# Three forms of an MLP's first product, and hidden layers cut in four pieces at twelve places, in a two-block transformer kernel

## The chip, the cores and the metric

The program runs on one core of one Trainium2 chip. The metric is the device time of one execution in microseconds (us); lower is better. The times below are of whole executions; the profile is of one more execution, whose instructions were recorded.

## The reference

Two transformer blocks in a row, on 256 tokens of width 1024, all in float32: the first with sparse attention, a linear recurrence and a short convolution, then the second with two layers, each an attention mixer and an MLP. So the program has three MLPs, and the change is in them and in where their operands lie. Cut to what matters:

```python
D_MODEL, SEQ, D_FF = 1024, 256, 4096

def first_block(x, ...):
    ...                                   # mixers, then x = x + mixed @ w_out
    h = _rmsnorm(x, ln_mlp_g)
    return x + jnp.square(jax.nn.relu(h @ w_mlp_up)) @ w_mlp_down

def second_block(x, ...):
    for layer in range(2):
        h = rmsnorm(x, norm_mix[layer])
        x = x + (even_mixer, odd_mixer)[layer](h, ...)
        h = rmsnorm(x, norm_mlp[layer])
        x = x + jnp.square(jax.nn.relu(h @ w_up[layer])) @ w_down[layer]
    return rmsnorm(x, norm_final)
```

## The kernel before

**Arithmetic.** Every large product is done in three parts: weights W and activations a are each split into a rounded high part (float32r) and the rest, and W·a is taken as h·ah + h·al + l·ah (h, l the parts of the weights, ah, al those of the activations). Activations lie transposed: 128 partitions by k (8 blocks of 128 for the width 1024, 32 for 4096) by 256 tokens. One matrix multiplication (matmul) takes a 128x128 block of weights as its stationary side and 256 or 512 columns of activations as its moving side.

**Weights.** They come from memory as one stream `w` in chunks of 16 blocks. `take` (L183) splits a unit of 8 blocks: ScalarE (ACT) writes `whi` (L193), VectorE (DVE) writes `wlo` in two halves (L195). Each of `whi` and `wlo` has five buffers of one unit, at fixed addresses.

**Forms of a product.** `gemm` (L246) makes one output tile of 128x256 with three matmuls for each k: L250 (h·ah), L253 (h·al), L254 (l·ah). `gemm2` makes two such tiles in one buffer `pg` of PSUM; there are four `pg`. `gemm_wide` (L257) has two matmuls for each k: L262 takes al behind ah as 512 columns in one matmul, L263 adds l·ah on 256 columns. The two halves of its result are then added: ACT copies one out (L412), DVE adds (L413).

**An MLP** (`mlp`, L379). First product: 32 output tiles, in 16 pairs by `gemm2` from `xo` (`xh`, `xl`), 8 k each; each pair goes through L395 (relu, ACT), L396 (square to the high part of `hid`, ACT), L397 and L398 (DVE: the low part of `hid`). Second product: 8 output tiles of 32 k from `hid`, seven by `gemm_wide`, the last by `gemm`. So each product has 256 steps of one k for one output tile. Before the first product `variance` (L380) sums squares into the one buffer `po` by matmuls (L347, L348), and DVE reads it (L382, L383). The three MLPs are called with `gain_next` = "norm_mix0" (the first block's), "norm_mix1" and `None`: here the first, second and third MLP.

**Places.** `xo` and `hid` are one tile each, with 128 elements more than they need (`ROOM`), and what is written into them starts some elements behind the tile's beginning: `PLACES` gives that for `xo` in each stage, `HIDDEN` for `hid` in each MLP. The tiles' own addresses do not change, so these numbers set how far the moving columns lie from the weights' buffers. In the stages named: "block1" is the first block's mixer, "ln_mlp_g" the first MLP's first product, "norm_mix0" the mixer behind it, "norm_mlp0" the second MLP, "norm_mix1" the last mixer, "norm_mlp1" the third MLP.

**Order.** Each engine works through its own queue in order. A scheduler that simulates the engines sets that order when the program is built.

Of the kernel before, what the change touches and what calls it, by code (L numbers as in the profile page):

```python
# [10 lines left out]
FP32 = mybir.dt.float32  # L11
FP32R = mybir.dt.float32r
# [3 lines left out]
ALU = mybir.AluOpType  # L16
# [27 lines left out]
ROOM = 128  # L44
PLACES = {"block1": 32, "ln_mlp_g": 64, "norm_mix0": 24, "norm_mlp0": 96, "norm_mix1": 20, "norm_mlp1": 0}
HIDDEN = {"norm_mix0": 16, "norm_mix1": 48, None: 8}
MIXED = 16
# [35 lines left out]
def kernel(  # L83
# [42 lines left out]
    def place(stage):  # L126

        nonlocal xh, xl
        at = PLACES[stage]
        xh, xl = placed(xo, KD, at), placed(xo, KD, at + KD * T)  # L130

# [110 lines left out]
    def drain():  # L242
        while due or chains:
            slot()

    def gemm(ps, ks, ah, al, prev=None):  # L246

        for k in ks:
            h, l = block()
            m0 = nc.tensor.matmul(out=ps, lhsT=h, rhs=ah[:, k], start=(k == ks[0]), stop=False)  # L250
            if k == ks[0]:
                after(m0, prev)
            nc.tensor.matmul(out=ps, lhsT=h, rhs=al[:, k], start=False, stop=False)  # L253
            m1 = nc.tensor.matmul(out=ps, lhsT=l, rhs=ah[:, k], start=False, stop=(k == ks[-1]))  # L254
        return m1

    def gemm_wide(kt, a):  # L257

        ps = pg_p.tile([128, 2, T], FP32, name="pg")
        for k in range(kt):  # L260
            h, l = block()
            nc.tensor.matmul(out=ps, lhsT=h, rhs=a[:, k], start=(k == 0), stop=False)  # L262
            nc.tensor.matmul(out=ps[:, 1], lhsT=l, rhs=a[:, k, 0], start=False, stop=(k == kt - 1))  # L263
        slot(kt / KD)
        return ps
# [100 lines left out]
    def residual(ah, al, groups, gain):  # L366


        for ks in groups[:-1]:
            for j in range(KD):  # L370
                nc.vector.tensor_tensor(out=x[:, j], in0=gemm1(ks, ah, al, RC), in1=x[:, j], op=ALU.add)
        drain()
        place(gain)
        for j in range(KD):
            nc.vector.tensor_tensor(out=x[:, j], in0=gemm1(groups[-1], ah, al), in1=x[:, j], op=ALU.add)
            operand(j, gain)
            squares(j)

    def mlp(gain_next):  # L379
        def variance():  # L380
# [5 lines left out]
        with ExitStack() as st:  # L386
            hp = pool("hid", stack=st)
            mp = pool("mlpt", 2, stack=st)
            hid = hp.tile([128, FF // 128 * 2 * T + ROOM], FP32R, name="hid")
            hid = placed(hid, FF // 128 * 2, HIDDEN[gain_next]).rearrange("p (k i) t -> p k i t", i=2)  # L390
            for j in range(0, FF // 128, 2):
                ps = gemm2(KD, xh, xl)
                r = mp.tile([128, 2, T], FP32, name="r")
                s = mp.tile([128, 2, T], FP32, name="s")
                nc.scalar.activation(out=r, in_=ps, func=AF.Relu)  # L395
                nc.scalar.activation(out=hid[:, j:j + 2, 0], in_=r, func=AF.Square)  # L396
                nc.vector.scalar_tensor_tensor(out=s, in0=ps, scalar=0.0, in1=r, op0=ALU.max, op1=ALU.mult)  # L397
                nc.vector.tensor_tensor(out=hid[:, j:j + 2, 1], in0=s, in1=hid[:, j:j + 2, 0], op=ALU.subtract)  # L398
            if gain_next is not None:
                place(gain_next)  # L400
            for j in range(KD):

                wide = j < KD - WN
                if wide:
                    ps = gemm_wide(FF // 128, hid)
                else:
                    ps = gemm1(FF // 128, hid[:, :, 0], hid[:, :, 1])

# [497 lines left out]
    with ExitStack() as st:  # L906
# [82 lines left out]
        for j in range(0, 8, 2):  # L989
# [4 lines left out]
            qk(f"e{j + 1}")  # L994
        residual(oh, ol, GROUPS_ATT, "norm_mlp0")
    mlp("norm_mix1")


# [349 lines left out]
```

## Time and profile before

| | |
|---|---|
| median of 3 runs | 1078.59 us (1076.27 to 1080.89) |
| the profiled execution | 1079.46 us, span of its instructions 1077.7 us |
| TensorE matmul (PE) busy | 1055.1 us, 98% of the span |
| TensorE weight load (PEld) busy | 1015.3 us, 94% |
| VectorE (DVE) busy | 836.2 us, 78% |
| ScalarE (ACT) busy | 602.0 us, 56% |

The span runs from the first to the last instruction. Busy time is the union of an engine's instructions. Matmuls overlap each other in the record, so the pace of TensorE is read from starts: the first and the last start of a line's matmuls in a stretch, divided by their count less one. In the first products that is the time of one k step (three matmuls, one of them on L250), in the second products that of one wide step (L262 and L263).

### The profile page before, as it was taken

The numbers are of one execution on the slowest core, as the hardware profiler recorded it, in microseconds if no ns is written. First come the engines' busy times: TensorE is split into PE (matmuls) and PEld (weight loads), VectorE is DVE, ScalarE is ACT, GpSimd is POOL, SyncE is SP. The second block draws the span as 40 slices with busy tenths as digits, with TensorE's granted clock in tenths as the row PEclk, the third lists the DMA queues.
The fourth block names the chain that finished last, engine by engine and source line by source line (L and its number), as shares of the span: only waits on it lengthen the run. The fifth ranks groups of instructions, "written<-read, shape, count | busy, mean of one in ns | idle before, by whom it ended". The sixth has DMA issues, their size and how long they took to land. (4 is left out here: it accounts for less than half of the span.)

```text
span 1077.7 us, 20317 instructions
## 1 busy us (share of the span) xinstructions
PE 1055.1 (98%) x8136; PEld 1015.3 (94%) x8136; DVE 836.2 (78%) x1613; ACT 602.0 (56%) x944; POOL 158.8 (15%) x174
## 2 busy tenths in 40 slices
PE   7999999999999999999999999999999999999996
PEld 7999989999999988899999999888999999999886
DVE  8999898887996666678778866667689788666663
ACT  6467456665575544456654655444458755555441
POOL 1045650110500001120003000011121022000110
PEclk9999999999999999999999999999999999999999
DMA  8544333545455555554433555554444334555541
GB/s 319 201 170 159 132 118 132 182 173 185 157 199 193 196 186 179 185 209 151 148 136 139 189 175 186 196 192 163 169 181 157 118 118 170 185 193 196 186 166 40
DMA packets 29007, 183.94 MB, mean 171 GB/s; under 512 B 3056, under 2 KB 6384, under 8 KB 7280
## 3 DMA queue, kind: packets, MB, share of 16 engines
q1 hardware_dynamic: 28768, 182.50, 47.5%
q8 instruction: 64, 1.05, 0.4%
q14 instruction: 31, 0.25, 0.1%
q10 hardware_dynamic: 144, 0.13, 0.0%
HBM read 181.57 MB, written 1.05 MB: 169 GB/s over the span
## 5 line engine op out<-in xcount | busy, mean ns | idle before, releaser
L195 DVE TENSOR_TENSOR wlo<-stg,whi 128x512 fp32r<-128x512 f32 (+1 forms) x676 | 470.8, 737 | 164.7 <-ACT whi L193 158.4
L193 ACT ACTIVATE whi<-stg 128x1024 fp32r<-128x1024 f32 (+1 forms) x340 | 356.0, 1050 | 333.8 <-PE pg L253 184.9
L250 PE MATMUL pg<-xo,whi 128*128 128x256 f32 x1472 | 415.7, 283 | 7.5 <-ACT whi L193 6.5
L254 PE MATMUL pg<-xo,wlo 128*128 128x256 f32 x1472 | 415.0, 282 | 0.4 <-DVE wlo L195 0.3
L253 PE MATMUL pg<-xo,whi 128*128 128x256 f32 x1472 | 414.4, 282 | 0.6 <-DVE xo L327 0.6
L250 PEld LDWEIGHTS pg<-xo,whi 128*128 128x128 f32 x1472 | 276.6, 188 | 8.9 <-ACT whi L193 6.8
L254 PEld LDWEIGHTS pg<-xo,wlo 128*128 128x128 f32 x1472 | 278.8, 190 | 1.7 <-DVE wlo L195 1.1
L253 PEld LDWEIGHTS pg<-xo,whi 128*128 128x128 f32 x1472 | 276.9, 188 | 2.1 <-DVE xo L327 1.3
L262 PE MATMUL pg<-hid,whi 128*128 128x512 f32 x672 | 235.1, 394 | 0.0
L263 PE MATMUL pg<-hid,wlo 128*128 128x256 f32 x672 | 188.9, 281 | 0.0
L262 PEld LDWEIGHTS pg<-hid,whi 128*128 128x128 f32 x672 | 126.3, 188 | 28.8
L263 PEld LDWEIGHTS pg<-hid,wlo 128*128 128x128 f32 x672 | 126.3, 188 | 0.0
L335 POOL TENSOR_TENSOR sqa<-xv 128x256 f32<-128x256 f32 x6 | 4.1, 677 | 468.3 <-DVE xv L415 302.8
L339 POOL TENSOR_TENSOR sq<-xv 128x256 f32<-128x256 f32 x36 | 28.3, 791 | 174.7 <-DVE xv L415 170.8
L289 PE MATMUL pg<-whi,xo 128*128 128x256 f32 x256 | 47.5, 283 | 0.0
L289 PEld LDWEIGHTS pg<-whi,xo 128*128 128x128 f32 x256 | 39.5, 188 | 0.1
L479 ACT ACTIVATE p<-p,m 128x128 f32<-128x128 f32 x64 | 28.6, 448 | 18.3 <-DVE m L477 18.3
L340 POOL TENSOR_TENSOR sqa<-sqa,sq 128x256 f32<-128x256 f32 x36 | 36.6, 1017 | 2.4
L253 PE MATMUL pg<-ol,whi 128*128 128x256 f32 x128 | 36.4, 286 | 0.2 <-DVE ol L299 0.2
L398 DVE TENSOR_TENSOR hid<-s,hid 128x512 fp32r<-128x512 f32 x48 | 33.2, 691 | 4.0
L254 PE MATMUL pg<-oh,wlo 128*128 128x256 f32 x128 | 36.1, 285 | 0.0
L289 PE MATMUL pg<-wlo,xo 128*128 128x256 f32 x128 | 36.0, 281 | 0.0
(356 smaller groups left out, 1540.1 us busy)
## 6 DMA issues: line engine op xcount, KB each, us to landing
stg<-w SPq DMA_DIRECT2D x168, 1024.0 KB, 4.8
t<-t_bias SPq DMA_DIRECT2D x8, 128.0 KB, 2.5
cb<-chk_bias SPq DMA_DIRECT2D x1, 1024.0 KB, 4.8
xv<-x_in SPq DMA_DIRECT2D x2, 384.0 KB, 5.9
cst<-consts SPq DMA_DIRECT2D x1, 640.0 KB, 10.6
stg<-w SPq DMA_DIRECT2D x1, 512.0 KB, 7.7
out<-xg SPq DMA_DIRECT2D x2, 256.0 KB, 2.5
stg<-w SPq DMA_DIRECT2D x1, 384.0 KB, 6.4
```

What stands on the lines that cost most here:

```text
L193: act = [nc.scalar.activation(out=h[:, z], in_=src[:, z], func=AF.Copy) for z in (pieces if u == 0 else [slice(0, UW)])]
L195: dve = [nc.vector.tensor_tensor(out=l[:, z], in0=src[:, z], in1=h[:, z], op=ALU.subtract) for z in pieces]
L250: m0 = nc.tensor.matmul(out=ps, lhsT=h, rhs=ah[:, k], start=(k == ks[0]), stop=False)
L253: nc.tensor.matmul(out=ps, lhsT=h, rhs=al[:, k], start=False, stop=False)
L254: m1 = nc.tensor.matmul(out=ps, lhsT=l, rhs=ah[:, k], start=False, stop=(k == ks[-1]))
L262: nc.tensor.matmul(out=ps, lhsT=h, rhs=a[:, k], start=(k == 0), stop=False)
L263: nc.tensor.matmul(out=ps[:, 1], lhsT=l, rhs=a[:, k, 0], start=False, stop=(k == kt - 1))
L289: nc.tensor.matmul(out=ps, lhsT=a[:, k, t], rhs=w_, start=(k == 0 and i == 0), stop=(k == kt - 1 and i == 2))
L339: nc.gpsimd.tensor_tensor(out=s, in0=x[:, j], in1=x[:, j], op=ALU.mult)
L340: nc.gpsimd.tensor_tensor(out=sqa, in0=sqa, in1=s, op=ALU.add)
L398: nc.vector.tensor_tensor(out=hid[:, j:j + 2, 1], in0=s, in1=hid[:, j:j + 2, 0], op=ALU.subtract)
L479: nc.scalar.activation(out=p[:, a:b], in_=p[:, a:b], func=AF.Exp, scale=-1.0, bias=m[:, i:i + 1], accum_out=sums[:, i:i + 1])
```

## The change

It edits four things. `PLACES` has other numbers. `hid` is cut in four pieces of eight k each: piece q starts 4128·q elements behind the tile's beginning (4096 of data and 32 between), plus its own number in `HIDDEN`, so that the starts are 4, 44, 88, 128 ahead of whole pieces in the first MLP, 2, 38, 74, 110 in the second and 1, 35, 82, 124 in the third. `gemm` can take l·ah ahead of h·al (`order`), and can issue one matmul of n columns into `po`, whose result nothing reads, ahead of each output tile (`between`). The first MLP's first product is made with the other order, the second's with `gemm_wide` (for which `place` lays `xo` out as pairs of ah and al), the third's with `between`.

```diff
-PLACES = {"block1": 32, "ln_mlp_g": 64, "norm_mix0": 24, "norm_mlp0": 96, "norm_mix1": 20, "norm_mlp1": 0}
-HIDDEN = {"norm_mix0": 16, "norm_mix1": 48, None: 8}
+PLACES = {"block1": 32, "ln_mlp_g": 32, "norm_mix0": 32, "norm_mlp0": 24, "norm_mix1": 40, "norm_mlp1": 32}
+BESIDE = "norm_mlp0"
+HIDDEN = {"norm_mix0": [4, 12, 24, 32], "norm_mix1": [2, 6, 10, 14], None: [1, 3, 18, 28]}
+BETWEEN = [16, 32, 48, 64, 80, 96, 112, 128]
...
         at = PLACES[stage]
+        if stage == BESIDE:
+            both = placed(xo, 2 * KD, at).rearrange("p (k i) t -> p k i t", i=2)
+            xh, xl = both[:, :, 0], both[:, :, 1]
+            return both
...
         for k in ks:
             h, l = block()
-            m0 = nc.tensor.matmul(out=ps, lhsT=h, rhs=ah[:, k], start=(k == ks[0]), stop=False)
+            if k == ks[0] and form["between"] is not None:
+                n = BETWEEN[form["n"] % len(BETWEEN)]
+                form["n"] += 1
+                after(nc.tensor.matmul(out=form["between"][:, 0:n], lhsT=h, rhs=ah[:, k, 0:n], start=True, stop=True), prev)
+            m0 = nc.tensor.matmul(out=ps, lhsT=h, rhs=tile_k(ah, k), start=(k == ks[0]), stop=False)
             if k == ks[0]:
                 after(m0, prev)
-            nc.tensor.matmul(out=ps, lhsT=h, rhs=al[:, k], start=False, stop=False)
-            m1 = nc.tensor.matmul(out=ps, lhsT=l, rhs=ah[:, k], start=False, stop=(k == ks[-1]))
+            rest = [(h, al), (l, ah)]
+            for i, (w_, a) in enumerate(rest[::-1] if form["order"] else rest):
+                m1 = nc.tensor.matmul(out=ps, lhsT=w_, rhs=tile_k(a, k), start=False, stop=(k == ks[-1] and i == 1))
...
-            hid = placed(hid, FF // 128 * 2, HIDDEN[gain_next]).rearrange("p (k i) t -> p k i t", i=2)
+            quarter = FF // 512
+            parts = [placed(hid_t, quarter * 2, q * (quarter * 2 * T + ROOM // 4) + at).rearrange(
+                "p (k i) t -> p k i t", i=2) for q, at in enumerate(HIDDEN[gain_next])]
+            form["order"] = gain_next == "norm_mix0"
+            if gain_next is None:
+                form["between"] = po_p.tile([128, 512], FP32, name="po")
             for j in range(0, FF // 128, 2):
-                ps = gemm2(KD, xh, xl)
...
+                if gain_next == "norm_mix1":
+                    ps = mp.tile([128, 2, T], FP32, name="sum")
+                    for i in range(2):
+                        pw = gemm_wide(KD, both)
+                        nc.scalar.activation(out=r[:, i], in_=pw[:, 1], func=AF.Copy)
+                        nc.vector.tensor_tensor(out=ps[:, i], in0=pw[:, 0], in1=r[:, i], op=ALU.add)
+                else:
+                    ps = gemm2(KD, xh, xl)
```

The order of instructions differs in the first products of the three MLPs alone. Three places of it follow; the line numbers of the changed kernel are new: L268 stands for L250, L273 for L253 and L254, L281 and L282 for L262 and L263, L204 for L195, L430 and L431 for L397 and L398; L423 and L424 are the new copy and add, L267 the matmul of `between`.

TensorE, in the middle of the second MLP's first product, before and then changed:

```order
L250 MATMUL pg<-xo,whi 128x256
L253 MATMUL pg<-xo,whi 128x256
L254 MATMUL pg<-xo,wlo 128x256
L250 MATMUL pg<-xo,whi 128x256
L253 MATMUL pg<-xo,whi 128x256
```

```order
L281 MATMUL pg<-xo,whi 128x512
L282 MATMUL pg<-xo,wlo 128x256
L281 MATMUL pg<-xo,whi 128x512
L282 MATMUL pg<-xo,wlo 128x256
L281 MATMUL pg<-xo,whi 128x512
```

The three matmuls of a step became two on as many columns, and each output tile has a `pg` of its own.

VectorE, one pair of tiles in the same place, before and then changed (`wlo` from `stg` is the split of weights, `sum` the new tile that holds a pair's result):

```order
L195 TENSOR_TENSOR wlo<-stg,whi 128x512 x4
L397 SCALAR_TENSOR_TENSOR s<-pg,r 128x512
L398 TENSOR_TENSOR hid<-s,hid 128x2x256
L195 TENSOR_TENSOR wlo<-stg,whi 128x512 x4
L397 SCALAR_TENSOR_TENSOR s<-pg,r 128x512
```

```order
L204 TENSOR_TENSOR wlo<-stg,whi 128x512 x2
L424 TENSOR_TENSOR sum<-pg,r 128x256
L204 TENSOR_TENSOR wlo<-stg,whi 128x512 x2
L424 TENSOR_TENSOR sum<-pg,r 128x256
L430 SCALAR_TENSOR_TENSOR s<-sum,r 128x512
L431 TENSOR_TENSOR hid<-s,hid 128x2x256
L204 TENSOR_TENSOR wlo<-stg,whi 128x512 x2
```

Two adds per pair stand among the splits now, and L430 reads `sum` in place of `pg`.

TensorE, in the third MLP's first product, between two output tiles of the changed kernel (before, L250 followed L254 there):

```order
L268 MATMUL pg<-xo,whi 128x256
L273 MATMUL pg<-xo,whi 128x256
L273 MATMUL pg<-xo,wlo 128x256
L267 MATMUL po<-xo,whi 128x32
L268 MATMUL pg<-xo,whi 128x256
```

One matmul of 16 to 128 columns came in between; there are 32 of these in all, and the first four of them stand in one row, behind the read of `po` by L402 (L382 before).

## Rows read from the trace of the kernel before

**Rows 1.** The page: the span, and busy time, share and instructions by engine.

```profile
span 1077.7 us, 20317 instructions
PE 1055.1 (98%) x8136; PEld 1015.3 (94%) x8136; DVE 836.2 (78%) x1613; ACT 602.0 (56%) x944; POOL 158.8 (15%) x174
PEclk9999999999999999999999999999999999999999
```

**Rows 2.** Waits of PE, whole span: us in total, times, longest.

```profile
PE pg L250 <- ACT whi L193: 6.5, 2, 5.0
PE sc L788 <- DVE mm L752: 1.0, 1, 1.0
```

**Rows 3.** L250 in the three first products: duration min/median/max, first and last start.

```profile
L250 PE MATMUL pg<-xo,whi x199: 281/281/281, 299.7 to 369.7; 128*128 128x256 f32 x199
...
L250 PE MATMUL pg<-xo,whi x198: 279/279/280, 600.0 to 669.7; 128*128 128x256 f32 x198
...
L250 PE MATMUL pg<-xo,whi x185: 281/281/281, 910.0 to 975.0; 128*128 128x256 f32 x185
```

**Rows 4.** L262 in the three second products, same columns.

```profile
L262 PE MATMUL pg<-hid,whi x210: 392/392/396, 379.9 to 452.8; 128*128 128x512 f32 x105
...
L262 PE MATMUL pg<-hid,whi x208: 397/397/398, 681.7 to 754.9; 128*128 128x512 f32 x104
...
L262 PE MATMUL pg<-hid,whi x209: 390/390/390, 982.7 to 1054.8; 128*128 128x512 f32 x105
```

**Rows 5.** L250 in two stretches of the first block's mixer, same columns.

```profile
L250 PE MATMUL pg<-xo,whi x48: 276/276/276, 31.4 to 47.4; 128*128 128x256 f32 x48
...
L250 PE MATMUL pg<-xo,whi x16: 280/280/282, 240.6 to 245.9; 128*128 128x256 f32 x16
```

**Rows 6.** L779, one burst of small matmuls, same columns.

```profile
L779 PE MATMUL sc<-mm x8: 222/222/270, 129.9 to 130.3; 128*64 128x64 f32 x8
```

**Rows 7.** Groups by line, 610 to 660 us, DVE and ACT: busy, mean ns, idle before.

```profile
L195 DVE TENSOR_TENSOR wlo<-stg,whi 128x512 fp32r<-128x512 f32 x36 | 23.4, 689 | 14.4 <-ACT whi L193 13.2
L398 DVE TENSOR_TENSOR hid<-s,hid 128x512 fp32r<-128x512 f32 x10 | 6.9, 692 | 0.9
L397 DVE SCALAR_TENSOR_TENSOR s<-pg,r 128x512 f32<-128x512 f32 x9 | 6.2, 684 | 0.0
...
L193 ACT ACTIVATE whi<-stg 128x1024 fp32r<-128x1024 f32 x18 | 19.1, 1060 | 21.4 <-PE pg L253 21.4
L396 ACT ACTIVATE hid<-r 128x512 fp32r<-128x512 f32 x9 | 5.7, 632 | 0.3
L395 ACT ACTIVATE r<-pg 128x512 f32<-128x512 f32 x9 | 5.2, 580 | 0.0
```

**Rows 8.** Groups by line, 700 to 750 us (second MLP's second product), DVE and ACT.

```profile
L195 DVE TENSOR_TENSOR wlo<-stg,whi 128x512 fp32r<-128x512 f32 x36 | 26.9, 787 | 17.1 <-ACT whi L193 17.1
L415 DVE TENSOR_TENSOR xv<-dn,xv 128x256 f32<-128x256 f32 x5 | 2.1, 427 | 0.5
L414 DVE TENSOR_TENSOR dn<-dn,rvar 128x256 f32<-128x256 f32 x5 | 2.1, 425 | 0.2
L413 DVE TENSOR_TENSOR dn<-pg,dn 128x256 f32<-128x256 f32 x5 | 2.1, 418 | 0.0
...
L412 ACT ACTIVATE dn<-pg 128x256 f32<-128x256 f32 x5 | 1.8, 366 | 0.0
```

**Rows 9.** Busy time in a stretch of the second MLP's first product: PE, PEld, DVE, ACT, POOL.

```profile
600.00:670.00 70.00, 70.00 (x597) 70.00 (x596) 51.34 (x81) 42.65 (x54) 0.00 (x0) 1.00 0.56 200
```

**Rows 10.** L250 in the mixers behind the first and second MLP, columns of rows 3.

```profile
L250 PE MATMUL pg<-xo,whi x127: 277/280/367, 468.8 to 557.2; 128*128 128x256 f32 x127
...
L250 PE MATMUL pg<-xo,whi x102: 277/280/474, 772.9 to 850.5; 128*128 128x256 f32 x102
...
L250 PE MATMUL pg<-xo,whi x18: 277/278/280, 787.9 to 793.8; 128*128 128x256 f32 x18
```

**Rows 11.** Timeline of DVE at the third MLP's start: start, us, instruction, idle before.

```profile
897.80 0.42 DVE L382 TENSOR_SCALAR rs_u<-po 128x256 f32<-128x256 f32 x1
898.26 1.75 DVE L383 RECIPROCAL rvar<-rs_u 128x256 f32<-128x256 f32 x1
```

More of the change, by code (lines that the diff above doesn't have):

```diff
@@ L244, in drain, with tile_k @@
             slot()
+    def tile_k(a, k):
+        return a[k] if isinstance(a, list) else a[:, k]
+    form = {"order": 0, "between": None, "n": 0}
     def gemm(ps, ks, ah, al, prev=None):
@@ L261, in gemm_wide @@
             h, l = block()
-            nc.tensor.matmul(out=ps, lhsT=h, rhs=a[:, k], start=(k == 0), stop=False)
-            nc.tensor.matmul(out=ps[:, 1], lhsT=l, rhs=a[:, k, 0], start=False, stop=(k == kt - 1))
+            nc.tensor.matmul(out=ps, lhsT=h, rhs=tile_k(a, k), start=(k == 0), stop=False)
+            nc.tensor.matmul(out=ps[:, 1], lhsT=l, rhs=tile_k(a, k)[:, 0], start=False, stop=(k == kt - 1))
         slot(kt / KD)
@@ L372, in residual @@
         drain()
-        place(gain)
+        both = place(gain)
         for j in range(KD):
@@ L377, in residual, with mlp @@
             squares(j)
-    def mlp(gain_next):
+        return both
+    def mlp(gain_next, both=None):
         def variance():
@@ L388, in mlp @@
             mp = pool("mlpt", 2, stack=st)
-            hid = hp.tile([128, FF // 128 * 2 * T + ROOM], FP32R, name="hid")
-            hid = placed(hid, FF // 128 * 2, HIDDEN[gain_next]).rearrange("p (k i) t -> p k i t", i=2)
+            hid_t = hp.tile([128, FF // 128 * 2 * T + ROOM], FP32R, name="hid")
+            quarter = FF // 512
[4 more added lines that the diff above has]
+                form["between"] = po_p.tile([128, 512], FP32, name="po")
             for j in range(0, FF // 128, 2):
-                ps = gemm2(KD, xh, xl)
                 r = mp.tile([128, 2, T], FP32, name="r")
                 s = mp.tile([128, 2, T], FP32, name="s")
+                if gain_next == "norm_mix1":
[6 more added lines that the diff above has]
+                    ps = gemm2(KD, xh, xl)
+                hid = parts[j // quarter][:, j % quarter:j % quarter + 2]
                 nc.scalar.activation(out=r, in_=ps, func=AF.Relu)
-                nc.scalar.activation(out=hid[:, j:j + 2, 0], in_=r, func=AF.Square)
+                nc.scalar.activation(out=hid[:, :, 0], in_=r, func=AF.Square)
                 nc.vector.scalar_tensor_tensor(out=s, in0=ps, scalar=0.0, in1=r, op0=ALU.max, op1=ALU.mult)
-                nc.vector.tensor_tensor(out=hid[:, j:j + 2, 1], in0=s, in1=hid[:, j:j + 2, 0], op=ALU.subtract)
+                nc.vector.tensor_tensor(out=hid[:, :, 1], in0=s, in1=hid[:, :, 0], op=ALU.subtract)
+            form.update(order=0, between=None)
+            hid_k = [parts[k // quarter][:, k % quarter] for k in range(FF // 128)]
             if gain_next is not None:
@@ L404, in mlp @@
                 if wide:
-                    ps = gemm_wide(FF // 128, hid)
+                    ps = gemm_wide(FF // 128, hid_k)
                 else:
-                    ps = gemm1(FF // 128, hid[:, :, 0], hid[:, :, 1])
+                    ps = gemm1(FF // 128, [a[:, 0] for a in hid_k], [a[:, 1] for a in hid_k])
                 for z in HALVES if gain_next is None and j == KD - 1 else [slice(0, T)]:
@@ L994 @@
             qk(f"e{j + 1}")
-        residual(oh, ol, GROUPS_ATT, "norm_mlp0")
-    mlp("norm_mix1")
+        both = residual(oh, ol, GROUPS_ATT, "norm_mlp0")
+    mlp("norm_mix1", both)
     first(rsqrt(sum_squares(), T, 1.0 / D, rstd))
```

## Prediction, made before the changed kernel ran

> **What bounds the kernel now.** I read the page first. TensorE is busy 98% of the span, at the full granted clock in every slice [rows 1], and the waits name 6.5 us as its longest item in 1077.7, the next 1.0 us [rows 2]. So time comes from TensorE's pace, step by step, and a neighbour's work matters only where it makes TensorE wait. I therefore went to the single lines and took their first and last starts, because the durations overlap. A k step of the first products takes 70.0/198 = 353.5 ns, 69.7/197 = 353.8 and 65.0/184 = 353.3 [rows 3]; a wide step of the second products 72.9/209 = 348.8, 73.2/207 = 353.6 and 72.1/208 = 346.6 ns [rows 4]. The same three matmuls take 16.0/47 = 340.4 ns in one stretch of the first mixer and 5.3/15 = 353 in another [rows 5], from the same place in `xo`: the reader should see two paces, 13 ns apart, and that the place alone does not choose between them. Six products of 256 steps make 1536 steps in all, so the whole change plays for 1536 x 13 ns = 20 us at most as far as pace goes.
>
> All sums are made against the profiled execution, 1079.46 us (1077.7 of span and 1.8 around it), which lies 0.9 us above the median of the runs, 1078.59. I call a change of over 0.5% (5.4 us) faster or slower; that is about what a measurement of this kernel can tell from none.
>
> **First MLP, first product: other order.** The same 768 matmuls on the same operands; only l·ah goes ahead of h·al. The place moves from 64 to 32, and "block1" at 32 shows both paces [rows 5]. Bounds: 256 x (353.5 - 340.4) = 3.4 us gained, or nothing. The stage ran 70 us at the slow pace without a change [rows 3], and so did the other two, at places 96 and 0; I take 0.
>
> **Second MLP, first product: wide.** 512 matmuls replace 768, on as many columns. No row shows this product wide; the nearest are the wide steps from `hid` [rows 4], at 346.6 (place 8), 348.8 (16) and 353.6 ns (48). The new place is 24; of the three, 8 is the only one that is also 8 beyond a multiple of 16, so I take 346.6: 256 x (353.8 - 346.6) = 1.8 us gained. Bounds: 353.6, nothing, and 340.4, 3.4 us.
>
> What it adds lies beside. A pair of output tiles takes TensorE 16 x 346.6 ns = 5.55 us. ACT gets two copies of 366 ns [rows 8]: 2 x 1060 + 2 x 366 + 580 + 632 = 4.1 us per pair [rows 7]. DVE gets two adds of 418 ns [rows 8]: 4 x 689 + 2 x 418 + 692 for L430, which now reads from `sum` like L398, + 692 = 4.98 us [rows 7]. That is 90% of the pair, against 51.34 of 70 us now [rows 9]; it is hidden while it stays under 5.55. Less is hidden at the start: each tile now takes a whole `pg`, so the four buffers hold four tiles where they held eight, while DVE still works off the operands of the mixer's end and has 1.75 us of reciprocal (L383 in [rows 11]) among its splits. Following the new DVE rows with these durations, the add that frees the first buffer of the third pair is done about 15.8 us after TensorE begins the MLP, and TensorE wants it, for the fourth pair, at 15.0. I add 0.8 us; bounds 0 and 2.
>
> **Third MLP, first product: a small matmul ahead of each tile.** 32 matmuls of 16 to 128 columns (mean 72), which nothing hides, since TensorE is the bound. The nearest row is L779: eight matmuls of few columns with 64 columns of weights start 0.4/7 = 57 ns apart [rows 6]. These here load 128 columns of weights, so I take twice that, 115 ns: 32 x 0.115 = 3.7 us. Bounds: 57 ns, 1.8 us; and the 118 ns of a 256-column matmul (353.5/3), 3.8 us.
>
> The Trainium skill ("TensorE: Matmul & The Clock Gate", Back-to-back issue gap) gives the gap between matmuls as their columns at 2.4 GHz and 2.5 ns. By it, as an estimate, 72 columns cost 32.5 ns and the 32 matmuls 1.0 us, and the whole sum would be 2.7 us less than with 3.7. The row speaks against it: 57 ns apart where that page would have some 25.
>
> The first four of them stand behind L402, since `po` is one buffer, and each reads a `whi`, so four of the five weight buffers stay held until then. DVE read `po` by 898.22 in the profile [rows 11]; in the new order 24 matmuls, 2.8 us, lie between the sum of squares and the first L267, so TensorE is not late there. Then a released buffer needs 1.06 us of ACT and 0.69 of DVE [rows 7], and TensorE has over 20 matmuls, 2.4 us, before it asks for that unit. I cost it at nothing; without that cover it would be one split, 1.75 us.
>
> **Second products.** Twelve pieces, 224 wide steps for each MLP. The new starts match none of the three places that rows show, so I take the mean of the three paces, 349.7 ns, for all: +0.2, -0.9 and +0.7 us, together 0. Bounds: all at 346.6, -2.1 us; all at 353.6, +2.6. DVE writes into the pieces at odd places; the nearest row is L415, which writes `xv` 78 elements behind its tile's start, 427 ns against L414's 425 [rows 8]: nothing.
>
> **Mixers.** Places 24 to 32 and 20 to 40: 127 and 102 steps on `xo`, now 5.9/17 = 347 ns in one stretch [rows 10], later between 340 and 353.5. From -1.5 to +1.5 us; I take 0.
>
> **Sum.** -1.8 + 0.8 + 3.7 = +2.7 us: 1082.2 in a profiled execution, 1081.3 as a median. The bounds that can hold together give 1076 to 1086 for this case.
>
> **Rivals.** *DVE becomes the bound in the second MLP's first product* (slower). The slack is 5.55 - 4.98 = 0.57 us per pair, and the add of the next tile now stands ahead of L430 in the queue: it waits for TensorE and an ACT copy. From 0.57 us of such waits per pair on, DVE decides; with 1.06 us, one split of weights on ACT in the way, 16 x 0.5 = 8 us come on top: 1089.3. For it: L195 takes 787 ns, not 689, beside other work [rows 8], which alone eats 0.39 us. Against it: POOL is idle there [rows 9], and five weight buffers are some 11 us of lead. Chance 0.10.
>
> *The fast pace is caught* (faster). Rows 5 show it held for 16 us once it is there, and after L267 each tile begins anew. If all steps ran at 340.4: 3.4 in each of the first and third first products, 1.6 in the second, 224 x (8.4 + 13.2 + 6.2) ns = 6.2 in the second products, 2 in the mixers, 16.6 us: 1064.7. Half of it gives 1073.0, where faster begins. Against it: all three first products kept the slow pace. Chance 0.10.
>
> *Distance does nothing*, and the paces of rows 4 came from something else: the wide product keeps 353.5 ns, and the sum is 0.8 + 3.7: 1083.1. For it: place 32 has both paces. Against it: each product holds its own pace for 70 us. Chance 0.20.
>
> The Trainium skill ("TensorE: Matmul & The Clock Gate", Step-by-step: what each phase is for) says that the two read ports are independent: "Loading the next tile's weights doesn't steal SBUF read bandwidth from the running matmul." By that rule distance from the weights is worth nothing. The trace does not quite agree: the same L262 lasts 390, 392 and 397 ns at three places [rows 4].
>
> *Odd starts cost a second read.* All places before are multiples of 4 elements; seven of the twelve pieces are not, two of them are odd. No row prices this for TensorE. If an odd start doubled a step, a piece would cost 64 x 0.347 = 22 us, two pieces 44: 1126. Against it: nothing in L415. Chance 0.05.
>
> **How the numbers follow.** The forecast has 0.55. Faster by over 0.5% (under 1073.2): 0.10, the second rival. Slower (over 1084.0): 0.10 + 0.05 and 0.03 from the forecast's upper end, 0.18. Same: 0.72. The range reaches to half of the fast rival and past the slow DVE one, 1070 to 1091; it leaves out the odd starts and the ends of those two, about 0.13.
>
> **What would show it.** Right: L268 353 ns a step in the first MLP; L281 about 347 in the second, DVE near 90% and PE without waits there; L267 115 ns from start to start, 3.7 us in all; the L281 of the second products between 346 and 354. Wrong: PE waiting for DVE (L204, L424) in the second MLP; steps of 340; any piece with steps far above 354.

## The result, and the profile after

The changed kernel took 1085.51 us (median of 4 runs, 1084.99 to 1086.19) against 1079.32 (4 runs, 1076.27 to 1080.89): a ratio of 1.0061, 95% interval 1.0037 to 1.0085. So it is slower than before, at the median by a little more than the 0.5% that I had asked of a change; the interval reaches below that. The forecast was 1081.3 us, and all four runs lie above 1084.0, where the prediction's "slower" begins; it had given that 0.18. The profiled execution has a span of 1083.3 us where before had 1077.7 [rows 1].

The page of the changed kernel, span and engines:

```profile
span 1083.3 us, 19909 instructions
PE 1061.5 (98%) x7912; PEld 1011.2 (93%) x7912; DVE 845.9 (78%) x1645; ACT 608.9 (56%) x976; POOL 158.2 (15%) x174
PEclk9999999999999999999999999999999999999999
```

TensorE is still busy 98% of the span at the full clock, so the time went into its pace again. The first k step's matmul in the three first products (columns of [rows 3]; L268 stands for L250, L281 is the wide matmul):

```profile
L268 PE MATMUL pg<-xo,whi x171: 280/280/280, 314.8 to 374.9; 128*128 128x256 f32 x171
...
L281 PE MATMUL pg<-xo,whi x174: 390/390/390, 609.8 to 669.7; 128*128 128x512 f32 x174
...
L268 PE MATMUL pg<-xo,whi x178: 278/280/366, 909.9 to 974.9; 128*128 128x256 f32 x178
```

A step takes 60.1/170 = 353.5 ns in the first MLP, as before. The wide one takes 59.9/173 = 346.2 ns, where the old form took 353.8 [rows 3]. In the third MLP it is 65.0/177 = 367 ns with the small matmuls counted in. The second products:

```profile
L281 PE MATMUL pg<-hid,whi x210: 387/392/398, 379.8 to 452.8; 128*128 128x512 f32 x105
...
L281 PE MATMUL pg<-hid,whi x208: 391/393/403, 681.9 to 754.7; 128*128 128x512 f32 x104
...
L281 PE MATMUL pg<-hid,whi x207: 388/398/404, 985.7 to 1058.7; 128*128 128x512 f32 x104
```

73.0/209 = 349.3, 72.8/207 = 351.7 and 73.0/206 = 354.4 ns a step, against 348.8, 353.6 and 346.6 [rows 4]. The third lost 7.8 ns on each of 224 steps, and its durations spread from 388 to 404 where before every one was 390.

VectorE and ScalarE in the second MLP's first product (groups, 610 to 660 us, then busy time in 600 to 670 us, columns of [rows 9]), and all waits of PE from 585 to 680 us:

```profile
L204 DVE TENSOR_TENSOR wlo<-stg,whi 128x512 fp32r<-128x512 f32 x37 | 23.9, 685 | 7.3 <-ACT whi L202 7.3
L424 DVE TENSOR_TENSOR sum<-pg,r 128x256 f32<-128x256 f32 x20 | 8.2, 416 | 0.0
...
600.00:670.00 70.00, 70.00 (x406) 62.05 (x405) 60.69 (x109) 49.09 (x79) 0.00 (x0) 1.00 0.58 206
...
PE pg L281 <- DVE xv L394: 0.6, 1, 0.6
```

VectorE rose from 51.34 to 60.69 us of 70, 87%, and TensorE waits for none of the new work: the 0.6 us is at the end of the mixer's residual (L394 adds it).

### The profile page after: what moved, and what is told of

Its sections match the earlier page's. It is cut to its first block, busy times and chain, and to the rows that moved or that the text cites. A ratio compares the mean times of both kernels' runs of the same rounds, so it can differ in the third digit from the quotient of the medians.

```text
span 1083.3 us, 19909 instructions
## 1 busy us (share of the span) xinstructions
PE 1061.5 (98%) x7912; PEld 1011.2 (93%) x7912; DVE 845.9 (78%) x1645; ACT 608.9 (56%) x976; POOL 158.2 (15%) x174
## 4 chain that ended last, share of the span: by engine, by line
PE 87%; DVE 8%; ACT 2%; issue 1%; POOL 1%; DMA 1%; SPq 0%; DVEq 0%; POOLq 0%
PE pg L273 30%; PE pg L281 20%; PE pg L268 15%; PE pg L282 10%; DVE wlo L204 3%; PE pg L308 3%; PE po L531 1%; PE sc L494 1%; PE pt L524 1%; ACT whi L202 1%; PE sc L487 1%; PE po L532 1%; DVE xo L346 1%; DMA stg<-w 1%; DVE xv L394 0%
## 5 line engine op out<-in xcount | busy, mean ns | idle before, releaser
L204 DVE TENSOR_TENSOR wlo<-stg,whi 128x512 fp32r<-128x512 f32 (+1 forms) x676 | 470.6, 738 | 145.5 <-ACT whi L202 144.4
L268 PE MATMUL pg<-xo,whi 128*128 128x256 f32 x1216 | 347.0, 286 | 6.6 <-ACT whi L202 6.2
L273 PE MATMUL pg<-xo,whi 128*128 128x256 f32 x1216 | 343.5, 283 | 0.6 <-DVE xo L346 0.6
L273 PE MATMUL pg<-xo,wlo 128*128 128x256 f32 x1216 | 343.1, 283 | 0.2
L268 PEld LDWEIGHTS pg<-xo,whi 128*128 128x128 f32 x1216 | 229.4, 189 | 7.7 <-ACT whi L202 6.5
L281 PE MATMUL pg<-hid,whi 128*128 128x512 f32 x672 | 236.4, 394 | 0.0
L273 PEld LDWEIGHTS pg<-xo,whi 128*128 128x128 f32 x1216 | 229.5, 189 | 2.0 <-DVE xo L346 1.3
L273 PEld LDWEIGHTS pg<-xo,wlo 128*128 128x128 f32 x1216 | 229.3, 189 | 1.3 <-DVE wlo L204 0.7
L282 PE MATMUL pg<-hid,wlo 128*128 128x256 f32 x672 | 189.1, 281 | 0.0
L281 PEld LDWEIGHTS pg<-hid,whi 128*128 128x128 f32 x672 | 126.8, 189 | 29.2
L282 PEld LDWEIGHTS pg<-hid,wlo 128*128 128x128 f32 x672 | 126.8, 189 | 0.0
L281 PE MATMUL pg<-xo,whi 128*128 128x512 f32 x256 | 89.1, 391 | 0.6 <-DVE xv L394 0.6
L282 PE MATMUL pg<-xo,wlo 128*128 128x256 f32 x256 | 72.0, 283 | 0.0
L281 PEld LDWEIGHTS pg<-xo,whi 128*128 128x128 f32 x256 | 47.9, 188 | 11.1 <-DVE xv L394 1.0
L282 PEld LDWEIGHTS pg<-xo,wlo 128*128 128x128 f32 x256 | 48.4, 189 | 0.2
```

Source lines behind the costliest of these rows:

```text
L204: dve = [nc.vector.tensor_tensor(out=l[:, z], in0=src[:, z], in1=h[:, z], op=ALU.subtract) for z in pieces]
L268: m0 = nc.tensor.matmul(out=ps, lhsT=h, rhs=tile_k(ah, k), start=(k == ks[0]), stop=False)
L273: m1 = nc.tensor.matmul(out=ps, lhsT=w_, rhs=tile_k(a, k), start=False, stop=(k == ks[-1] and i == 1))
L281: nc.tensor.matmul(out=ps, lhsT=h, rhs=tile_k(a, k), start=(k == 0), stop=False)
L282: nc.tensor.matmul(out=ps[:, 1], lhsT=l, rhs=tile_k(a, k)[:, 0], start=False, stop=(k == kt - 1))
```

## Experiments

All are read by the same stages, from the starts of TensorE's matmuls: a first product runs from the last matmul of the mixer's residual to the first large one on `hid`, a second product from there to its last on `hid`, a mixer from there to the next first product. Times in us of the profiled executions; the columns are before, the changed kernel (chg), and experiments 1 to 11 below.

| stage | before | chg | 1 | 2 | 3 | 4 | 5 | 6 | 7 | 8 | 9 | 10 | 11 |
|---|---|---|---|---|---|---|---|---|---|---|---|---|---|
| mixer 1 | 283.50 | 285.11 | 284.95 | 283.56 | 284.38 | 285.13 | 284.20 | 284.37 | 284.53 | 284.98 | 284.75 | 284.25 | 284.84 |
| 1st MLP, first | 92.21 | 92.24 | 92.19 | 92.20 | 92.20 | 92.95 | 92.32 | 94.25 | 92.24 | 90.98 | 92.69 | 92.49 | 89.80 |
| second | 89.35 | 89.56 | 89.34 | 89.34 | 89.35 | 89.56 | 89.34 | 90.63 | 90.65 | 88.74 | 88.75 | 90.33 | 88.75 |
| mixer 2 | 120.52 | 120.20 | 120.51 | 120.48 | 120.48 | 120.20 | 120.52 | 120.52 | 119.98 | 120.52 | 120.51 | 120.52 | 120.52 |
| 2nd MLP, first | 92.97 | 90.94 | 92.96 | 92.99 | 91.03 | 90.93 | 90.45 | 94.29 | 90.93 | 91.00 | 90.40 | 92.06 | 90.39 |
| second | 90.33 | 90.18 | 90.33 | 90.33 | 90.32 | 90.18 | 90.33 | 90.68 | 89.55 | 88.74 | 88.75 | 90.33 | 88.75 |
| mixer 3 | 117.30 | 117.95 | 117.24 | 117.21 | 117.13 | 117.85 | 117.27 | 117.28 | 117.87 | 117.36 | 117.28 | 117.35 | 117.34 |
| 3rd MLP, first | 92.69 | 96.38 | 92.79 | 95.18 | 92.86 | 92.87 | 91.49 | 89.70 | 92.83 | 90.86 | 90.13 | 90.94 | 90.29 |
| second | 88.75 | 90.65 | 88.75 | 88.74 | 88.74 | 90.70 | 88.75 | 89.74 | 90.48 | 88.74 | 88.75 | 88.74 | 88.75 |

My theory after the result: each part has a price of its own, set by how its moving columns lie to the weights, and the sum of the parts is the loss. The rival: paces come and go from execution to execution, and part of the loss is that.

**1. Before once more** (no edit).

> The kernel before, profiled a second time. Theory A (the paces come and go from execution to execution): the k steps of the first block's mixer from 31 to 47 us, 340 ns in the first profile, come out elsewhere between 340 and 353, and the span moves by 1 us or more from 1077.7 (the runs so far spread over 4.6 us). Theory B (program and places set the pace): the same steps again at 340 ns, the three first products at 353.5 and the second products at 348.8, 353.6 and 346.6 ns a step, and a span within 0.5 us of 1077.7.

Ratio 0.9995 (0.9983 to 1.0007). Span 1079.1 us, 1.4 above the first profile, and all of that is in mixer 1; the other stages repeat to 0.1 us. Two stretches of L250 in mixer 1, here:

```profile
L250 PE MATMUL pg<-xo,whi x46: 276/276/276, 32.0 to 47.3; 128*128 128x256 f32 x46
...
L250 PE MATMUL pg<-xo,whi x21: 280/280/280, 115.6 to 123.3; 128*128 128x256 f32 x21
```

the second stretch in the first profile of before:

```profile
L250 PE MATMUL pg<-xo,whi x23: 276/276/276, 115.5 to 123.0; 128*128 128x256 f32 x23
```

and the first one in the changed kernel:

```profile
L268 PE MATMUL pg<-xo,whi x46: 279/279/279, 31.6 to 47.5; 128*128 128x256 f32 x46
```

The duration is the mark of the pace: 276 goes with 340 ns a step (15.3/45, 7.5/22 = 341), 279 and 280 with 353 (15.9/45; 7.7/20 = 385 is more because four matmuls of another product stand between, 0.65 us). One program had the stretch from 115 us at one pace in one execution and at the other in the next. So in these two profiles theory B holds for the MLPs (experiments 6 and 9 will show stages of MLPs that change too), and theory A for mixer 1, where no code was changed: over all thirteen profiles it took 283.50 to 285.13 us, and the profile that I had predicted from was the lowest.

**2. The small matmuls alone**, with `PLACES` and `HIDDEN` of before:

```diff
+                after(nc.tensor.matmul(out=form["between"][:, 0:n], lhsT=h, rhs=ah[:, k, 0:n], start=True, stop=True), prev)
             m0 = nc.tensor.matmul(out=ps, lhsT=h, rhs=tile_k(ah, k), start=(k == ks[0]), stop=False)
```

> The kernel before with nothing but the small matmuls ahead of the output tiles in the third MLP's first product; places and pieces as before. If each costs what it did in the changed kernel (3.69 us for 32), that stage takes 96.4 us in place of 92.7 and the whole 3.7 us more, 0.3%. If it also costs what follows it (the changed kernel's second product behind it took 90.65 us, 1.90 more than before), the second product is longer as well: 5.6 us more. Rival: the small matmuls shift the phase of the steps and the whole gains or loses nothing, within 1 us of before.

Ratio 1.0029 (1.0017 to 1.0040). The second product is untouched, but the first costs 2.49 us, not 3.7, and neither theory had that. TensorE's timeline around two of them, ahead of a tile with 112 columns and of one with 128 (start, duration, instruction):

```profile
928.94 0.28 PE L273 MATMUL pg<-xo,wlo 128*128 128x256 f32 x1
929.05 0.21 PE L267 MATMUL po<-xo,whi 128*128 128x112 f32 x1
929.11 0.34 PE L268 MATMUL pg<-xo,whi 128*128 128x256 f32 x1
929.28 0.28 PE L273 MATMUL pg<-xo,whi 128*128 128x256 f32 x1
...
931.89 0.22 PE L267 MATMUL po<-xo,whi 128*128 128x128 f32 x1
931.95 0.33 PE L268 MATMUL pg<-xo,whi 128*128 128x256 f32 x1
932.12 0.28 PE L273 MATMUL pg<-xo,whi 128*128 128x256 f32 x1
...
934.83 0.17 PE L267 MATMUL po<-xo,whi 128*128 128x16 f32 x1
```

From one L267 to the next, 25 matmuls: 2.84 us behind 112 columns, 2.94 behind 128. Matched start by start over the last three rounds of sizes, the tiles behind 112, 96 and 48 columns ran at 113.3 to 114.3 ns per matmul, three matmuls in 340 ns, and all others at 117.8, each round alike. At place 32, in the changed kernel, no size did that. So a small matmul can start the fast pace, and there it nearly pays for itself: 24 x 4.5 = 108 ns. One of another size can end it too: 128 columns follow the fast tile behind 112, and the tile behind them is slow again.

**3. The wide form alone**, in the second MLP; all else as before.

```diff
-"norm_mlp0": 96
+"norm_mlp0": 24
-                ps = gemm2(KD, xh, xl)
+                    for i in range(2):
+                        pw = gemm_wide(KD, both)
```

> The kernel before with nothing but the second MLP's first product in the wide form, at place 24. If the form and the place give it, that stage takes 90.9 us in place of 93.0 and the whole 2.0 us less, 0.2%. Rival: the gain came with another place of the mixers beside it, and alone it is within 0.5 us of before. VectorE stays below 90% of that stage and TensorE does not wait for it, in either case.

Ratio 0.9984 (0.9971 to 0.9997); the stage 91.03 us, as expected, and no other stage but mixer 1 moved by over 0.2.

**4. The changed kernel without the small matmuls:**

```diff
-            if gain_next is None:
-                form["between"] = po_p.tile([128, 512], FP32, name="po")
```

> The changed kernel without the small matmuls; all else as changed. If they cost 3.7 us and no more, the third MLP's first product goes from 96.4 to 92.7 us, its second product stays at 90.6, and the whole is 3.7 us below the changed kernel: about 1.9 us above before by the profiles. If the second product's 1.9 us came with them, it goes back to 88.8 as well, and the whole is level with before.

Ratio to before 1.0023 (1.0013 to 1.0033). First product 92.87, second 90.70: the 1.9 us did not come with the small matmuls. (The first MLP's 92.95 is 0.7 us of start-up, over when the sum of squares ends at 291.8 us; from there on its steps are as in the changed kernel.)

**5. Few small matmuls, place 0 in all MLPs.** The list gives the columns of the matmul ahead of each of the 32 tiles, 0 for none; all else as before:

```diff
+SMALL = {
+    "norm_mix0": ([112 if j == 4 else 0 for j in range(32)], []),
+    "norm_mix1": ([112 if j % 8 == 4 else 0 for j in range(32)], []),
+    None: ([112 if j >= 4 and j % 2 == 0 else 0 for j in range(32)], []),
+}
```

> The kernel before with all three first products at place 0 and small matmuls of 112 columns only ahead of few output tiles: in the first MLP ahead of one tile (the fifth), in the second ahead of four, in the third ahead of fourteen (every second from the fifth on). With the small matmuls alone, at place 0, the tiles behind 112 columns ran at 113.3 ns per matmul in place of 117.8. Theory A (the fast pace is held until something disturbs it, as in the first block's mixer for 16 us): 27 or 28 tiles of 24 matmuls gain 4.5 ns each, 3.0 us, less 0.11 us for each small matmul: first MLP's first product about 89.3 us (from 92.2), second 90.4 (from 93.0), third 91.2 (from 92.7); 7 us less in all, 1073. Theory B (it lasts to the end of the tile): each small matmul gives back what it costs, and all stages stay within 0.3 us of before.

Ratio 0.9981 (0.9968 to 0.9995). The step's first matmul (L275 here) in the three first products:

```profile
L275 PE MATMUL pg<-xo,whi x185: 281/281/281, 309.7 to 374.8; 128*128 128x256 f32 x185
...
L275 PE MATMUL pg<-xo,whi x161: 276/276/338, 621.8 to 676.5; 128*128 128x256 f32 x161
...
L275 PE MATMUL pg<-xo,whi x189: 276/276/338, 909.7 to 974.9; 128*128 128x256 f32 x189
```

In the second MLP 54.7/160 = 341.9 ns with three small matmuls counted in: the fast pace is held until the stage ends. The third's 65.2/188 = 346.8 is 340 and 0.11 us for every 16 steps. The first MLP did not catch it. Theory A, two times in three.

But the three starts are not alike. In the second and third MLP the first small matmul came later than the list says, and an l·ah matmul follows it; in the first MLP h·ah follows. The second MLP, then the first (start, duration, instruction):

```profile
602.46 0.21 PE L265 MATMUL po<-xo,whi 128*128 128x112 f32 x1
602.52 0.34 PE L280 MATMUL pg<-xo,wlo 128*128 128x256 f32 x1
...
297.26 0.21 PE L265 MATMUL po<-xo,whi 128*128 128x112 f32 x1
297.31 0.34 PE L275 MATMUL pg<-xo,whi 128*128 128x256 f32 x1
```

It is so in experiments 9 and 11 as well. In experiment 2 each tile behind 112 columns follows a fast one, behind 96. So no run shows 112 columns with h·ah behind them start the fast pace at place 0, and the MLP and what follows the small matmul were not tried apart there.

**6. Small matmuls elsewhere:** sizes 16 to 128 in turn ahead of tiles in the first MLP (place 64), the second (wide, place 24), and ahead of all second products' tiles; none in the third's first product.

```diff
+    "norm_mix0": ([16 * (1 + j % 8) if j >= 4 else 0 for j in range(32)], [16 * (1 + j) for j in range(8)]),
+    "norm_mix1": ([16 * (1 + j % 8) if j >= 4 else 0 for j in range(32)], [16 * (1 + j) for j in range(8)]),
+    None: ([0] * 32, [16 * (1 + j) for j in range(8)]),
```

> Small matmuls of 16 to 128 columns ahead of tiles where none stood: in the first MLP's first product at place 64, in the second's in the wide form at place 24 (both from the fifth tile on), and ahead of the eight output tiles of each second product, places 16, 48 and 8 as before. Theory A (a small matmul of the right size starts the fast pace at any place, and the size differs by place): some tiles of each stage run at 113 ns per 256 columns, three matmuls or their like in 340 ns. Theory B (only place 0 has it): no tile does, and each small matmul costs its 0.11 us: 28 x 0.11 = 3.1 us in each of the two first products and 0.9 in each second product, 8.9 us in all, less 2.0 for the wide form: 1086.5.

Ratio 1.0060 (1.0039 to 1.0080). At place 64 the same three sizes, 48, 96 and 112, had the fast pace behind them, ten tiles of 28 (all of the last three rounds), and the others not. That stage had come in fast by itself: its steps took 340 ns from the sum of squares on, until the first small matmul, of 80 columns, at 297.2 us; behind it they were slow. L275 ahead of that matmul and behind it:

```profile
L275 PE MATMUL pg<-xo,whi x12: 276/276/276, 292.9 to 296.9; 128*128 128x256 f32 x12
...
L275 PE MATMUL pg<-xo,whi x8: 281/281/356, 297.3 to 299.8; 128*128 128x256 f32 x8
```

No wide tile gained anything, and there the price stood alone (94.29 - 91.0 = 3.3 us for 28). So neither theory holds for all: A for the old form at place 64, B for the wide one. The surprise was the third MLP, which had no small matmul:

```profile
L275 PE MATMUL pg<-xo,whi x201: 276/276/276, 910.0 to 978.0; 128*128 128x256 f32 x101
```

68.0/200 = 340.0 ns throughout, from the sum of squares at 903 us on; the stage took 89.70 us. So the stage at place 0, 92.7 to 92.9 in the three other profiles that have it at place 0 without small matmuls, can fall into the fast pace by itself.

**7. The pieces dealt to other MLPs**, on the kernel of experiment 4:

```diff
-HIDDEN = {"norm_mix0": [4, 12, 24, 32], "norm_mix1": [2, 6, 10, 14], None: [1, 3, 18, 28]}
+HIDDEN = {"norm_mix0": [1, 3, 18, 28], "norm_mix1": [4, 12, 24, 32], None: [2, 6, 10, 14]}
```

> The changed kernel without the small matmuls, and with the twelve pieces of the hidden layers dealt to other MLPs: the third MLP's four starts (1, 35, 82, 124) in the first MLP, the first's (4, 44, 88, 128) in the second, the second's (2, 38, 74, 110) in the third. If the start decides the pace, it goes with the pieces: steps of 358 and 360 ns behind starts 1 and 82 now in the first MLP, whose second product gets 1.1 us longer than the changed kernel's 89.6, the second's 0.6 shorter than 90.2 and the third's 0.5 shorter than 90.7. If it hangs on the MLP, the three keep 89.6, 90.2 and 90.7 and each piece keeps the pace of the piece that lay there.

Ratio to before 1.0036 (1.0021 to 1.0050). Second products 90.65, 89.55 and 90.48 us: the third MLP's pieces took their loss to the first MLP. But the third gained only 0.2 us by losing them, where 0.5 was expected. One tile's wide matmuls on the pieces that start at 1, 35, 82 and 124, in the changed kernel's third MLP:

```profile
L281 PE MATMUL pg<-hid,whi x9: 392/400/404, 1016.2 to 1019.0; 128*128 128x512 f32 x9
...
L281 PE MATMUL pg<-hid,whi x9: 390/390/403, 1019.0 to 1021.8; 128*128 128x512 f32 x9
...
L281 PE MATMUL pg<-hid,whi x9: 390/398/403, 1021.8 to 1024.7; 128*128 128x512 f32 x9
...
L281 PE MATMUL pg<-hid,whi x9: 388/397/403, 1024.7 to 1027.5; 128*128 128x512 f32 x9
```

and in the first MLP of this kernel:

```profile
L281 PE MATMUL pg<-hid,whi x9: 392/400/404, 410.4 to 413.2; 128*128 128x512 f32 x9
...
L281 PE MATMUL pg<-hid,whi x9: 390/390/403, 413.2 to 416.0; 128*128 128x512 f32 x9
```

Matched start by start, the mean steps of these four pieces (56 each) are 358.3, 346.7, 359.8 and 351.3 ns in the changed kernel and within 0.2 ns of that here. The first MLP's four moved as exactly. The four that went to the third MLP did not: 354.3, 353.6, 348.8 and 350.6 became 352.9, 352.8, 355.2 and 352.2.

**8. All wide:** all first products by `gemm_wide` at place 24, all hidden layers whole at 8.

```diff
-BESIDE = "norm_mlp0"
+BESIDE = ("ln_mlp_g", "norm_mlp0", "norm_mlp1")
-HIDDEN = {"norm_mix0": [4, 12, 24, 32], "norm_mix1": [2, 6, 10, 14], None: [1, 3, 18, 28]}
+HIDDEN = {"norm_mix0": [8] * 4, "norm_mix1": [8] * 4, None: [8] * 4}
```

> What the runs point to: all three first products in the wide form at place 24, all hidden layers whole at place 8, no small matmuls, the mixers at the places of before. If form and place give the wide step 346.6 ns wherever it is used: first products 2.0 us less each in the second and third MLP and 1.3 to 2 in the first, second products 0.5 (16 to 8) and 1.6 (48 to 8) less: some 7 us below before, 1073. Rival: VectorE, with two adds more per pair, holds up the first or third MLP's start, and half of it is lost: 1076.

1073.41 us, ratio 0.9960 (0.9946 to 0.9974). All three first products gained (1.23, 1.97, 1.83 us), the second ones 0.61 and 1.59: 7.2 us, as expected. The whole gained less, 4.0 us between the medians (before 1077.41 beside it); mixer 1 took 1.48 us more than in the first profile of before. The first of the three rows, which read alike:

```profile
L281 PE MATMUL pg<-xo,whi x189: 390/390/390, 309.7 to 374.9; 128*128 128x512 f32 x189
```

65.2/188 = 346.8 ns.

**9. Few small matmuls and whole hidden layers at 8**, on the kernel of experiment 5; in each of the three MLPs:

```diff
+    "norm_mix0": ([112 if j in (3, 5, 9, 17) else 0 for j in range(32)], []),
```

> The kernel before with all first products at place 0 in their old form, small matmuls of 112 columns ahead of four tiles in each (the fourth, sixth, tenth and eighteenth), and all hidden layers whole at place 8. If a small matmul starts the fast pace and nothing ends it within the stage, each first product gains 2.3 to 2.6 us (as the second MLP's did with four, 90.45 from 92.97), the second products 0.6 and 1.6 as with all at place 8: 9 to 10 us below before, 0.85 to 0.9%, and 1 to 2 below the kernel with all three in the wide form. Rival: the start is chance, as in the first MLP where one small matmul did nothing; then the stage that misses it keeps 92.6 and the gain is 6 to 7 us.

1073.78 us, ratio 0.9964 (0.9951 to 0.9976). The second and third MLP ran at the fast pace (90.40, 90.13), the first again did not and paid 0.48 us. The stages of the MLPs gained 6.8 us, the rival's number; the medians differ by 3.4 (before 1077.20), and mixer 1 took 1.25 more than in the first profile. In the third MLP the small matmuls started nothing: its steps were fast ahead of the first of them, at 897.44 us, too,

```profile
L275 PE MATMUL pg<-xo,whi x5: 276/276/276, 895.6 to 897.2; 128*128 128x256 f32 x5
```

and 90.13 is the 89.70 of experiment 6 and 4 x 0.11 us.

**10. The wide form at other places**, on the kernel of experiment 8, with the hidden layers at 16, 48 and 8:

```diff
-"ln_mlp_g": 24, "norm_mlp0": 24, "norm_mlp1": 24
+"ln_mlp_g": 16, "norm_mlp0": 48, "norm_mlp1": 8
```

> All three first products in the wide form, at places 16, 48 and 8, where the hidden layers lay in the kernel before; the hidden layers again at 16, 48 and 8. If the place sets the pace of a wide step, as the prediction took it, the first products run at 348.8, 353.6 and 346.6 ns a step, and the second MLP's stage takes 1.8 us more than at place 24 (92.8 in place of 91.0). If the form alone does it, all three stay at 346.6 and the stages at 91.0, 91.0 and 90.9.

Ratio 1.0016 (1.0007 to 1.0025). L281 in the three first products:

```profile
L281 PE MATMUL pg<-xo,whi x186: 395/398/403, 309.6 to 375.0; 128*128 128x512 f32 x186
...
L281 PE MATMUL pg<-xo,whi x171: 387/396/398, 619.6 to 679.3; 128*128 128x512 f32 x171
...
L281 PE MATMUL pg<-xo,whi x189: 392/392/392, 909.6 to 974.8; 128*128 128x512 f32 x189
```

65.4/185 = 353.5 ns at place 16, 59.7/170 = 351.2 at 48, 65.2/188 = 346.8 at 8. So the form alone does not give 346.6, and the place matters, as 8 and 24 against 16 and 48 show. But the pace at 16 and 48 is not that of `hid` at the same numbers, and `hid` at 16 itself, 89.35 us in before, took 90.33 here: the place alone does not fix it either.

**11. The first MLP at place 64**, with 48, 112 and 112 columns ahead of tiles 4, 6 and 16:

```diff
-"ln_mlp_g": 0
+"ln_mlp_g": 64
-    "norm_mix0": ([112 if j in (3, 5, 9, 17) else 0 for j in range(32)], []),
+    "norm_mix0": ([{4: 48, 6: 112, 16: 112}.get(j, 0) for j in range(32)], []),
```

> The kernel with few small matmuls and whole hidden layers, with one edit: the first MLP's first product at place 64, as before the change, with small matmuls of 48, 112 and 112 columns ahead of its fifth, seventh and seventeenth tile (at place 0 four of 112 columns had left it at the slow pace, 92.69 us). Theory A (place and size decide whether a small matmul starts the fast pace: at place 64 each tile behind 48 or 112 columns had it): the stage takes about 89.8 us, the other stages stay, and the whole is 2.5 to 2.9 us below that kernel, some 10 below before, 1067 to 1069 against a before of 1077 to 1080. Theory B (whether it starts there is chance): the stage stays near 92.6, and the whole at 0.36% below before.

1071.20 us, ratio 0.9925 (0.9911 to 0.9938), the fastest, though 2 us over the expected 1067 to 1069. The first MLP's first product took 89.80 us, the number of theory A:

```profile
L275 PE MATMUL pg<-xo,whi x186: 276/276/338, 309.9 to 372.9; 128*128 128x256 f32 x186
```

63.0/185 = 340.5 ns. But not all as thought: the 48 columns left its tiles slow here, and the 112 two tiles later started the pace.

## Why the prediction was right and wrong

My theory stands for most of the loss: the wide form alone (-1.94) and the small matmuls left out (3.51) have nearly the prices that they have in the changed kernel, and the slow pieces kept theirs in another MLP. It does not stand whole: the small matmuls alone, at place 0, cost 2.49, and the pieces of the second MLP went at other paces in the third. The order and the places of the first product in the first MLP were not tried apart. The rival stands for mixer 1, and experiments 6 and 9 show it for old first products at places 0 and 64, though not for the two profiles of before. The stages of the table account for the span: 0.03 - 2.03 + 3.69 + (0.21 - 0.15 + 1.90) + (-0.32 + 0.65) + 1.61 = 5.6 us, where I had summed 2.7. That is 2.9 of the 4.2 us by which the median missed the forecast; the rest is about that I took 0.9 off for a profile above the median, and here the profile lies 0.5 below it. The time stayed in the range, past the 1076 to 1086 of the likeliest case in two of its four runs. That was in part luck: the range reached to 1091 for a VectorE that becomes the bound, and the time came there for other reasons.

**What bounds.** Right: TensorE at full clock, hardly a wait, and every part of the result is pace.

**First MLP, other order: 0.** Measured 0.03.

**Second MLP, wide: -1.8 and +0.8.** The first term was right (-2.03 in the stage, -1.94 alone). Its reason, that place 24 would go like place 8, held in every run; in experiments 8 and 10 both are at 346.8. The stall of 0.8 us did not come: PE's longest wait there is the 0.6 us that before has too. My working had it one pair early. With four buffers of one tile each, the first buffer of the third pair, the fifth tile's, comes round for the ninth tile, in the fifth pair and not the fourth; the add that freed it ended at 611.08 us, and the ninth tile began at 611.49. VectorE at 87% is near what I had worked out (90%), and it hid.

**Third MLP, small matmuls: +3.7.** Measured 3.69, 3.51 against experiment 4. The size was right and its reason was not: I had doubled the 57 ns of L779 [rows 6]. In the changed kernel, a tile behind 16 columns:

```profile
935.41 0.28 PE L273 MATMUL pg<-xo,wlo 128*128 128x256 f32 x1
935.52 0.17 PE L267 MATMUL po<-xo,whi 128*128 128x16 f32 x1
935.55 0.37 PE L268 MATMUL pg<-xo,whi 128*128 128x256 f32 x1
935.75 0.28 PE L273 MATMUL pg<-xo,whi 128*128 128x256 f32 x1
```

Matched by starts, 16 columns start 26 ns ahead of the next matmul, which then holds for 203; 128 columns 60 and 168. Both sums are 228 to 229, that is 111 more than the 117.8 of a matmul alone: whatever its columns, the small one takes nearly the slot of a 256-column one, my upper bound. The estimate from the Trainium skill ("TensorE: Matmul & The Clock Gate", Back-to-back issue gap), 32.5 ns each and 1.0 us in all, does not hold for such matmuls between long ones. That section gives the formula for a matmul by itself and says that it under-counts small ones in a stream with weight loads, which I had left out; the trace agrees, with 111 ns.

**Second products: 0.** Measured 0.21 - 0.15 + 1.90 = +1.96. This is the step that failed: "I take the mean of the three paces, 349.7 ns, for all", with the fastest and the slowest of three places as bounds. Two of twelve starts, 1 and 82, ran at 358 and 360 ns, beyond both bounds and with the sign of being wrong that I had named (a piece far above 354), and the third MLP lost 1.90 us. The sum of the three stayed within its bound of +2.6. Experiment 7 shows the same paces, within 0.2 ns, at these starts in another MLP. A start does not always fix the pace: 74 went from 348.8 to 355.2. Three places were a sample, not limits; and the third MLP left the fastest known of them, so a loss there (+0.7 by my mean) was to be expected, and only its size was open. An odd start as such costs little: 35 is odd and at 346.7 ns. Why 1 and 82 are slow is open.

**Mixers: 0.** Measured -0.32 and +0.65, repeated in experiments 4 and 7 with the same places and absent wherever the places were those of before.

**Not in the sum: the profile that it starts from.** Mixer 1, unchanged, is 1.61 us longer than in the profile of before, and 1.45 longer in before's own second profile. I had read both paces there [rows 5], but not asked what my base would lose if the fast stretches did not come again. Before's median was 1079.32 here and 1077.20 to 1080.20 beside the experiments, its single runs 1074.42 to 1081.39, while the four of the changed kernel lie within 1.2 us. Old first products that come in fast by themselves, up to 3.0 us each, may be why; no profile of such an execution of before was taken, so that is not shown.

**Rivals.** VectorE did not become the bound. Odd starts did not double a step. "Distance does nothing" fell with experiments 7 and 10; the Trainium skill's rule ("TensorE: Matmul & The Clock Gate", Step-by-step: what each phase is for), that loading weights takes nothing from the running matmul, does not account for 346.8 against 353.5 ns by place alone. The fast pace was not caught by the changed kernel, but that rival was the live one: at places 0 and 64 it gives 2.4 to 3.0 us per first product, and with the third MLP at 32 the 32 small matmuls did not start it.

## What to carry to other kernels

Where one engine is the bound and hardly waits, compare its pace per step in each stage with the best pace that the same instructions show anywhere; here 340 against 353 ns was worth more than any form of the product. Move operands by a few elements and measure each place alone, and do not bound an unknown place by the few that a trace happens to show. Take a second profile of the kernel before: a stage that changes without an edit belongs in the range. And where an edit is to have started something, see in the trace that it had not begun ahead of it.

## What the runs showed of the hardware

- A stream of the same 256-column matmuls, at the full granted clock, runs at 113.3 or 117.8 ns each and keeps to one of the two, for 68 us in experiment 6. What comes ahead bears on which one: a small matmul of 112 columns started the fast one at place 0 in the second and third MLP, and not in the first, with `xo` at the same place (experiments 5, 9 and 11). What makes that difference is open; an l·ah matmul followed where it started, h·ah in the first MLP.
- The pace ahead of the sum of squares bears on it as well. Of the 19 old first products at places 0 and 64 in the profiles, 15 have their last matmuls ahead of its end at 113.2 to 113.5 ns, and all 15 run at 117.7 to 117.8 behind it; four have them at 117.5 to 118.0, and three of these run at 113.3 to 113.4 behind it (experiment 6 twice, experiment 9), one at 117.8 (experiment 3). At places 32 and 96 all nine have 117.5 to 118.0 ahead and 117.7 to 117.8 behind. No edit tried this, so the cause is not shown.
- Ahead of a tile, sizes 48, 96 and 112 had it behind them at places 0 and 64 (not every time: 48 failed in experiment 11), and behind each of the other sizes, alone ahead of a tile, it was slow, even where the pace had been fast (80 in experiment 6, 128 in experiment 2); at place 32 none of the eight sizes started it.
- Wide steps at places 8 and 24 ran at 346 to 347 ns wherever no small matmul stood among them. At place 16 the same second product took 89.35 or 90.33 us, so there the place alone does not choose.
